# A hybrid decoder step on one core: another order for the end of the QKV projection, the attention loop and the start of the output projection

## The chip, the core and the metric

The kernel runs on one core of a Trainium2 chip. The core has five engines, each working through its own instructions in order: TensorE (PE, with its weight loads shown as PEld), VectorE (DVE), ScalarE (ACT), GpSimd (POOL) and SyncE (SP). DMA transfers are issued from the queues of SP, ACT and POOL and run beside the engines. The metric is the device time of one execution in microseconds (us), as the median of several.

## The reference, cut to what matters

One inference step of a two-layer decoder: a prompt of 512 tokens and 8 sample sequences of 8 tokens with a past of 2048, D = 1024. Layer 0 is attention in three head groups `gi` with (window, dilation) = (128, 1), (512, 4), (2048, 16); layer 1 is a state-space (SSM) layer; each is followed by a SwiGLU feed-forward (FFN).

```python
qkv = (h @ w_qkv).reshape(B, T, 3, N_DIL, N_HEAD_SLOTS, HEAD_DIM)
q = rope(rmsnorm(qkv[:, :, 0], q_gain), pos)
k = rope(rmsnorm(qkv[:, :, 1], k_gain), pos)
v = qkv[:, :, 2]
...
s = jnp.einsum('bqhd,bqkhd->bqhk', q_blk, kf) * (HEAD_DIM ** -0.5)   # keys at distance 0, d, .., window
s = jnp.where(valid, s, -jnp.inf); lse = logsumexp(s); p = exp(s - lse)
o = jnp.einsum('bqhk,bqkhd->bqhd', p, vf)
...
wts = softmax(stack(lses)); o = sum over groups of wts * o           # merged per head slot
return o @ w_o, new_bufs
```

For the samples the old keys and values come from caches in HBM; new keys and values go to output caches. Everything is float32: a product is three TensorE products of high and low halves, high x high, high x low and low x high.

## The kernel before, in words

**Projection.** `qkv_phase` computes the nine chunks of `CHUNKS`, each a (part, group) of 512 columns with part 0 = q, 1 = k, 2 = v; the last is (2, 1). A chunk has four steps of two 128-row slices of `w_qkv`, so there are 36 steps, numbered j = 0 to 35 (`turn[0]`). In a step (`qkv_chunk`) TensorE runs six 128x512 matmuls for each of four tiles t = 0..3 of prompt rows and four for t = 4, the sample rows, into five accumulators `acc`. After each tile a `slot()` runs whatever was put there with `later(ahead, fn)`, `ahead` slots on; a step has five slots.

At the start of step j `begin()` puts on SP's queue, in this order: the weights of step j+2; the cached keys that `SCORES[j]` lists by group (0 or 1), to be worked on in step j; the pairs that `PAIRS` lists for step j+1. A pair is a tile of cached keys of group 2 and the queries spread over 128 partitions (`kc<-qscr`), 512 KB each; VectorE multiplies and reduces them one step later into a table P. Every fourth pair completes a sequence, and `Close2.turn` transposes P. `begin` also splits the weights of step j+1 into `whi` (ScalarE) and `wlo` (VectorE). The tiles of keys and pairs come from one pool, `kst`, of six buffers.

Keys of groups 0 and 1 are transposed on TensorE (`Score.turn`, into `pt`), copied by ScalarE (`ks`), and multiplied with the queries (`Score.dots`). All decode scores pass through one PSUM bank `Sd`; a row of it is 128 old keys and 8 new ones, and it is evicted with mask and maximum by VectorE:

```python
v.tensor_tensor_reduce(Sall[:, self.b, self.gi, :], Sd, md[:, self.gi, :], 1.0, -3e38, OP.add, OP.max, mx3[:, self.b, self.gi:self.gi + 1])
```

There are 24 such rows, eight sequences by three groups. `Kept` keeps all these operations in program order on their engine; because it records them, they all bear its line (L688) in the profile.

**Attention.** `attn_phase` loops over n = 0..19. For n < 16 it takes block n of the prompt (head pair n // 4, row class n % 4): `scores` (into `S`), `masked` (VectorE), `exps` (ScalarE), one turn later `turn` and `evict` (transposes through `pt` into P0 and P12), one more turn later `values`: products P12 with the values of groups 1 and 2 (`vt[1]`, `vt[2]`), and at the end of a head pair P0 with those of group 0 (`vt[0]`) and the reciprocal denominators R. `att` is a ScalarE copy of the values, multiplied by R on VectorE. Two turns carry one sample sequence (`Decode`): softmax, transposes, then products with 13 tiles of cached values (`cache_tile`, loaded through SP into `kst` and four more buffers) and one of new values `vn`.

**Output.** `wo_phase` splits `att` into `ath` (ScalarE) and `atl` (VectorE), multiplies with `w_o` in four chunks of 256 columns (`mm6`: six 128x288 matmuls for each slice) and adds the residual `xr`, read back from HBM in one load, into `xT`. Three pairs of banks `acc` take turns. FFN 0 follows, with `ssm_setup` beside it, whose loads (`ssm_a_re`, `ssm_log_dt`, `ssm_c_re` as `cw`, `ssm_b_re` as `bw`) stand on SP's queue around that of `xr`. Operations that are not kept in order are put in order by a scheduler.

The functions around it, with the profile's line numbers:

Of the kernel before, what the change touches and what calls it, by code (L numbers as in the profile page):

```python
# [18 lines left out]
D = 1024  # L19
T = 512  # L20
# [31 lines left out]
def _build(nc, tc, A, es):  # L52
# [71 lines left out]
    with ExitStack() as qs:  # L124
# [7 lines left out]
        md = dsp.tile([128, 3, 136], BF16, name="md")  # L132
        kst = rs_.enter_context(right("kst", bufs=KST))
# [80 lines left out]
    with ExitStack() as p3:  # L214
        wo_phase(nc, tc, A, p3, locals())
# [117 lines left out]
def qkv_chunk(nc, L, x, begin, step, pre=None, slot=None):  # L333
# [7 lines left out]
    for kk in range(4):  # L341
        wh, wl = begin()
        for t in range(4):
            if pre is not None:
                pre(kk, t)
            for k2 in range(2):
                k = kk * 2 + k2
                ah, al = x.h[:, k, t * 128:(t + 1) * 128], x.l[:, k, t * 128:(t + 1) * 128]
# [5 lines left out]
        for k2 in range(2):  # L354
            k = kk * 2 + k2
            mm(ps[4], x.s[:, k, :], wh[:, k2, :], start=k == 0, stop=False)
            mm(ps[4], x.s[:, k, :], wl[:, k2, :], start=False, stop=k == KT - 1)
        if slot is not None:
            slot()
# [32 lines left out]

class Close2:
    def __init__(self, nc, L, v, dk, psp, nm, P, b):
        self.nc, self.L, self.v, self.psp, self.nm, self.P, self.b = nc, L, v, psp, nm, P, b
# [7 lines left out]
    def turn(self):  # L403
# [8 lines left out]
        self.v.tensor_tensor_reduce(L["Sall"][:, b, 2, :], Sd, L["md"][:, 2, :], 1.0, -3e38, OP.add, OP.max, L["mx3"][:, b, 2:3])  # L412


def qkv_phase(nc, tc, A, es, L):
# [77 lines left out]
    def begin():  # L493
# [25 lines left out]
        for b, part, kc, qb in due:  # L519
# [6 lines left out]
            if part == 3:  # L526
                c = Close2(nc, L, v, dk, psd, "Sd", prods.pop(b), b)
                later(10, lambda c=c: close(c))
        return splits.pop(0)

    class Score:
# [23 lines left out]
        def dots(self, us):  # L555
# [14 lines left out]
            v.tensor_tensor_reduce(Sall[:, self.b, self.gi, :], Sd, md[:, self.gi, :], 1.0, -3e38, OP.add, OP.max, mx3[:, self.b, self.gi:self.gi + 1])  # L570
# [20 lines left out]
    def qk_chunk(gi, part):  # L591
# [17 lines left out]
        def finish(t, ahead):  # L609
# [9 lines left out]
            if t == 4 and part == (gi < 2):  # L619
# [23 lines left out]
    def v_chunk(gi, wk, vt=None):  # L643
        ps = qkv_chunk(nc, L, x, begin, step, None, slot)
        for t in range(5):
# [9 lines left out]
            kv_out(nc, A, gi, 1, t, a)  # L655

# [12 lines left out]
    def values():  # L669
        nc.sync.dma_start(vt0, L["vtscr"].rearrange("t p c -> p t c"))  # L670
        nc.sync.dma_start(mp, A["c_mp"])

    notes[34] = values
    with ExitStack() as e4:
        v_chunk(1, e4.enter_context(pool("wk2")), vt1)
# [3 lines left out]
    return [vt0, vt1, vt2], mp  # L679
# [11 lines left out]
def attn_phase(nc, tc, A, es, L):  # L691
# [20 lines left out]
    den, rd, S2, PT, sm, P0, P12, O = {}, {}, {}, {}, {}, {}, {}, {}  # L712

    def scores(n):
# [4 lines left out]
        for b in range(4):  # L719
            for h in range(2):  # L720
                o, k = S2[n][h][b * 32:b * 32 + 32, 0:256], kT[0][half[h], hp, max(b - 1, 0) * 128:(b + 1) * 128]
                if not b:
                    o, k = o.rearrange("p (a c) -> p a c", a=2), k[:, None, :].to_broadcast([64, 2, 128])
                mm(o, qT[0][half[h], hp, r * 128 + b * 32:r * 128 + b * 32 + 32], k, start=True, stop=True, tile_position=(h * 64, b * 32))
        sl = slice(r * 128, r * 128 + 128)
        for gi in (1, 2):
            for h in range(2):
                mm(S2[n][h][:, (gi + 1) * 128:(gi + 2) * 128], qT[gi][half[h], hp, sl], kT[gi][half[h], hp, sl], start=True, stop=True)
# [7 lines left out]
    def exps(n, h):  # L736
        x, nm = sm[n][h]
        s.activation(x, x, AF.Exp, bias=nm, scale=-1.0, accum_out=den[n // 4][:, n % 4, h:h + 1])
# [23 lines left out]
    def values(n):  # L762
# [8 lines left out]
        if r < 3:  # L771
            return
        for b in range(4):
# [6 lines left out]
        R = pS.tile([128, 512], F32, name="S")  # L780
        for c in range(4):
            for j in range(4):
                mm(R[j * 32:j * 32 + 32, c * 128:c * 128 + 128], rd[hp][:, c, j // 2:j // 2 + 1].to_broadcast([128, 32]), ident,
                   start=True, stop=True, tile_position=(0, j * 32))
        av = att[:, hp, :T].rearrange("p (b i r) -> p r b i", b=4, r=4)
        s.activation(av, o_, AF.Copy)
        v.tensor_tensor(av, av, R.rearrange("p (r b i) -> p r b i", r=4, b=4), OP.mult)
# [3 lines left out]
    class Decode:  # L791
        def __init__(self, b):
            self.b, self.u = b, 0
            P = Sall[:, b].rearrange("p a b -> p (a b)")
            nm, dn, rd = (dk.tile([128, 1], F32, name=x, bufs=2) for x in ("dnm", "ddn", "drd"))
            v.tensor_reduce(nm, mx3[:, b, :], AX.X, OP.max)
            v.tensor_scalar(nm, nm, -SCALE, None, op0=OP.mult)
            s.activation(P, P, AF.Exp, bias=nm, scale=SCALE, accum_out=dn)
            v.reciprocal(rd, dn)
            v.tensor_scalar(P, P, rd, None, op0=OP.mult)  # L800
            self.pw = dk.tile([128, 24], F32, name="pw")
            v.tensor_copy(self.pw.rearrange("p (a b) -> p a b", a=3), Sall[:, b, :, 128:136])
            self.vn = dk.tile([24, 512], F32, name="vn", bufs=2)
            nc.sync.dma_start(self.vn, dram(vscr, b * 8 * 512, [[64 * 512, 3], [512, 8], [1, 512]]))
# [19 lines left out]
        def values(self, part):  # L824
            b, Z = self.b, Pz[self.b % 2]
            if part == 0:
                self.O = pD.tile([128, 128], F32, name="Sd")
                for hp in range(4):
                    mm(self.O[hp * 32:hp * 32 + 32, :], self.pn[:, hp * 32:hp * 32 + 32], self.vn[:, hp * 128:hp * 128 + 128], start=True, stop=False, tile_position=(0, hp * 32))
            for gi, c0 in (((0, 0), (1, 0), (1, 2)), ((2, 0), (2, 2), (2, 4), (2, 6)))[part]:  # L830
                w = min(2, UNITS[gi] - c0)
                turns[0] += 1
                vc = cache_tile(nc, A, kst if turns[0] % 10 < KST else kp, "kc", gi, b, c0, w, 1)
                for c in range(w):
                    for hp in range(4):
                        pz = self.pa[:, hp, :] if self.u == 0 else Z[:, self.u - 1, hp, :]
                        mm(self.O[hp * 32:hp * 32 + 32, :], pz, vc[:, c, hp * 128:hp * 128 + 128], start=False, stop=self.u == 12, tile_position=(0, hp * 32))
                    self.u += 1
            if part == 0:
                return  # L840
            self.os = dk.tile([128, 128], F32, name="os")
# [9 lines left out]
    dec = {}  # L851
    for n in range(20):
# [643 lines left out]
```

## Time and profile before

| what | us |
|---|---|
| median of 3 runs (lowest, highest) | 1522.9 (1522.62, 1525.23) |
| the profiled execution | 1525.21 |
| its span, first to last instruction | 1523.4 |
| projection, by the trace | 0 to 319.5 |
| attention loop | 319.5 to 418 |
| output projection begins | 419.5 |
| mean granted TensorE clock | 0.993 of full |

How to read the rows that follow. Waits are "engine tile line <- engine tile line that released it: us in total, times, longest". Time rows are "start, length, engine, line, operation, out<-in", then partitions by elements and types, how many like it stand together, and in brackets the idle time before and who ended it. A stretch has busy time and count of each engine, then granted clock, busy share of the 16 DMA engines, and GB/s. A DMA row names the queue and, where it is a group, KB each and us from issue to landing.

### The profile page before, as it was taken

Reading aid. Unit: us, or ns where it says so; the run is one execution under the profiler, and the core shown is the slowest. Engines: PE = TensorE matmul, PEld = TensorE weight load, DVE = VectorE, ACT = ScalarE, POOL = GpSimd, SP = SyncE. Lnnn points to the kernel's source line nnn. Section 1 sums busy time; section 2 is a strip of 40 time slices with the busy share of each in tenths; the row PEclk is TensorE's granted clock in tenths of the full one; section 3 lists DMA queues with packets and bytes.
Section 4 is the critical chain, followed back from the end, with each engine's and each line's share of the span. In section 5 each row is a group of like instructions: output and inputs, shape, how many; then the busy total and the mean of one; then the engine's idle time right before and its main releaser. Section 6 shows DMA issues by size and latency. Waiting matters only on the chain. (4 is left out here: it accounts for less than half of the span.)

```text
span 1523.4 us, 29540 instructions
## 1 busy us (share of the span) xinstructions
PE 1480.0 (97%) x12406; PEld 1388.4 (91%) x12406; DVE 910.8 (60%) x1507; ACT 520.9 (34%) x790; POOL 315.2 (21%) x369
## 2 busy tenths in 40 slices
PE   9999999789999999999999999999999999999998
PEld 7877777557799999999999999899999999999998
DVE  5899988545467853688887568754443333333332
ACT  4523445345553221222123363432332212221222
POOL 2021132310031019544434330020110001000100
PEclk9999999979999999999999999999999999999999
DMA  7568587979775555797666828865546555442222
GB/s 253 190 242 299 187 288 236 345 261 311 256 231 191 194 199 195 243 302 257 240 242 238 301 97 252 267 206 191 190 164 221 190 191 192 149 151 89 83 63 76
DMA packets 190460, 322.62 MB, mean 212 GB/s; under 512 B 39480, under 2 KB 137016, under 8 KB 188792
## 3 DMA queue, kind: packets, MB, share of 16 engines
q1 hardware_dynamic: 182808, 303.63, 58.3%
q10 hardware_dynamic: 4992, 10.04, 1.9%
q0 software_dynamic: 2528, 7.08, 1.3%
q8 instruction: 97, 1.59, 0.4%
q14 instruction: 35, 0.29, 0.1%
HBM read 289.22 MB, written 118.78 MB: 268 GB/s over the span
## 5 line engine op out<-in xcount | busy, mean ns | idle before, releaser
L107 PE MATMUL acc<-xgl,whi 128*128 128x288 f32 x1760 | 378.6, 296 | 1.0 <-DVE xgl L172 1.0
L107 PE MATMUL acc<-xgh,wlo 128*128 128x288 f32 x1760 | 377.7, 296 | 0.0
L107 PE MATMUL acc<-xgh,whi 128*128 128x288 f32 x1760 | 377.1, 296 | 0.1
L101 DVE TENSOR_TENSOR wlo<-raw,whi 128x1024 fp32r<-128x1024 f32 (+1 forms) x168 | 207.6, 1236 | 238.1 <-ACT whi L100 234.8
L100 ACT ACTIVATE whi<-raw 128x1024 fp32r<-128x1024 f32 (+1 forms) x168 | 174.5, 1039 | 458.6 <-PE acc L107 404.8
L107 PEld LDWEIGHTS acc<-xgl,whi 128*128 128x128 f32 x1760 | 282.6, 188 | 2.5 <-DVE xgl L172 1.3
L107 PEld LDWEIGHTS acc<-xgh,wlo 128*128 128x128 f32 x1760 | 282.7, 188 | 0.6 <-issue 0.2
L107 PEld LDWEIGHTS acc<-xgh,whi 128*128 128x128 f32 x1760 | 281.8, 188 | 0.5 <-DVE gt L933 0.3
L935 POOL TENSOR_TENSOR gt<-gt,rstd 128x576 f32<-128x576 f32 x44 | 77.1, 1754 | 431.1 <-ACT gt L934 431.0
L107 PE MATMUL acc<-hh,whi 128*128 128x288 f32 x704 | 151.4, 296 | 0.0
L107 PE MATMUL acc<-hh,wlo 128*128 128x288 f32 x704 | 151.2, 295 | 0.0
L107 PE MATMUL acc<-hl,whi 128*128 128x288 f32 x704 | 151.0, 295 | 0.0
L337 PE MATMUL acc<-whi,xh 128*128 128x512 f32 x288 | 119.7, 417 | 1.2 <-ACT a L688 0.7
L107 PEld LDWEIGHTS acc<-hh,wlo 128*128 128x128 f32 x704 | 113.2, 188 | 0.2 <-issue 0.2
L107 PEld LDWEIGHTS acc<-hl,whi 128*128 128x128 f32 x704 | 113.0, 188 | 0.2 <-issue 0.2
L337 PE MATMUL acc<-wlo,xh 128*128 128x512 f32 x288 | 113.1, 394 | 0.0
L107 PEld LDWEIGHTS acc<-hh,whi 128*128 128x128 f32 x704 | 113.1, 188 | 0.0
L337 PE MATMUL acc<-whi,xl 128*128 128x512 f32 x288 | 112.3, 395 | 0.0
L192 POOL TENSOR_TENSOR ssum<-ssum,sq 128x576 f32<-128x576 f32 x21 | 36.2, 1723 | 232.4 <-ACT sq L191 232.4
L337 PEld LDWEIGHTS acc<-whi,xh 128*128 128x128 f32 x288 | 54.6, 190 | 12.3 <-ACT a L688 1.7
L337 PEld LDWEIGHTS acc<-whi,xl 128*128 128x128 f32 x288 | 54.6, 190 | 12.1
L947 DVE TENSOR_TENSOR xT<-acc,xT 128x576 f32<-128x576 f32 x48 | 36.2, 754 | 48.1 <-PE acc L107 48.1
(362 smaller groups left out, 2015.9 us busy)
## 6 DMA issues: line engine op xcount, KB each, us to landing
o_kv_s<-cache_kv_w SPq DMA_DIRECT2D x64, 1020.0 KB, 7.5
kc<-cache_kv_w SPq DMA_DIRECT2D x96, 512.0 KB, 6.7
raw<-ffn_w_gate SPq DMA_DIRECT2D x44, 512.0 KB, 3.6
raw<-ffn_w_up SPq DMA_DIRECT2D x44, 512.0 KB, 3.6
raw<-ffn_w_down SPq DMA_DIRECT2D x40, 512.0 KB, 3.4
raw<-w_qkv SPq DMA_DIRECT2D x36, 512.0 KB, 6.5
kc<-qscr SPq DMA_DIRECT2D x32, 512.0 KB, 6.1
o_kv_s<-cache_kv_w SPq DMA_DIRECT2D x16, 1008.0 KB, 6.1
```

Source lines behind the costliest of these rows:

```text
L100: s.activation(hi, raw, AF.Copy)
L101: mark[0] = v.tensor_tensor(lo, raw, hi.bitcast(F32), OP.subtract)
L107: te.matmul(ps[:, c, :HN], w, x[:, c * HN:(c + 1) * HN], start=first and i == 0, stop=last and i == 2)
L192: g.tensor_tensor(self.ss, self.ss, sq, OP.add)
L337: ins = nc.tensor.matmul(*a, **kw)
L935: g.tensor_tensor(t, t, nin.r, OP.mult)
L947: v.tensor_tensor(xv, ps[m][:, :, :HN], xv, OP.add)
```

## The change

It does six things. ScalarE copies a row of `Sd` to SBUF, and VectorE masks it there. `PAIRS` and `SCORES` get other numbers, and two sequences of group 0 share one load. In the last chunk the sample rows go first, each tile is evicted right behind its last matmul, and between the evictions stand the softmax of sequence 0 and the scores, masks and exponentials of block 0 (in the projection's `pt` banks and two `kst` tiles). The mask `mp` and the values `vt0` are loaded in steps 34 and 35 after everything else; new values `vn` are loaded from POOL's queue and multiplied last. Two of the four `w_o` loads are put at n = 11 and 13, the denominators' copy and the last sequence's output go ahead of the P0 products. And the output projection begins with all high parts of its first chunk, with `xr` in four loads; two copies of `ssm_setup` are held behind it.

```diff
-PAIRS = {7: 1, 9: 1, 10: 1, 11: 1, 12: 2, 13: 2, 14: 2, 15: 2, 17: 1, 18: 1, 19: 1, 21: 1, ... 31: 1, 32: 2, 33: 2, 34: 2}
+PAIRS = {7: 1, 8: 1, 10: 1, 11: 1, 12: 2, 13: 2, 14: 1, 15: 1, 18: 1, 19: 1, 20: 1, ... 23: 2, ... 27: 2, ... 31: 2, 32: 2, 33: 2, 34: 1}
...
+def row_out(v, s, L, Sd, b, gi):
+    o = L["Sall"][:, b, gi, :]
+    s.activation(o, Sd, AF.Copy)
+    v.tensor_tensor_reduce(o, o, L["md"][:, gi, :], 1.0, -3e38, OP.add, OP.max, L["mx3"][:, b, gi:gi + 1])
...
-                later(10, lambda c=c: close(c))
+                later(6 if j > 31 else 10, lambda c=c: close(c))
...
-        nc.sync.dma_start(vt0, L["vtscr"].rearrange("t p c -> p t c"))
-        nc.sync.dma_start(mp, A["c_mp"])
-    notes[34] = values
+    notes[34] = lambda: kept(nc.sync.dma_start(mp, A["c_mp"]))
+    notes[35] = lambda: kept(nc.sync.dma_start(vt0, L["vtscr"].rearrange("t p c -> p t c")))
...
+    def then(t):
+        if t == 4:
+            row_soft(v, s, Sall, mx3, 0, *soft)
+        if t == 0:
+            ...
+            score_block(lambda *a, **kw: kept(te.matmul(*a, skip_group_check=True, **kw)), S0, qT, kT, 0)
+            ...
+            for h in range(2):
+                v.tensor_tensor_reduce(sm0[h][0], S0[h], mp[:, 0, :], -SCALE, 3e38, OP.add, OP.min, sm0[h][1])
+        if t == 2:
+            for h in range(2):
+                s.activation(sm0[h][0], sm0[h][0], AF.Exp, bias=sm0[h][1], scale=-1.0, accum_out=den0[:, 0, h:h + 1])
...
-        v_chunk(1, e4.enter_context(pool("wk2")), vt1)
+        v_chunk(1, e4.enter_context(pool("wk2")), vt1, (4, 0, 1, 2, 3), then)
...
-        s.activation(av, o_, AF.Copy)
-        v.tensor_tensor(av, av, R.rearrange("p (r b i) -> p r b i", r=4, b=4), OP.mult)
+        s.activation(av, R.rearrange("p (r b i) -> p r b i", r=4, b=4), AF.Copy)     # ahead of the P0 products
+        between()
...
+        v.tensor_tensor(av, av, o_, OP.mult)
...
-            nc.sync.dma_start(self.vn, dram(vscr, b * 8 * 512, [[64 * 512, 3], [512, 8], [1, 512]]))
+            g.dma_start(self.vn, dram(vscr, b * 8 * 512, [[64 * 512, 3], [512, 8], [1, 512]]))
...
+    wo = L["split_w"](raws[0], s, v)
+    dec[7].values(1)
+    values(15, dec[7].out)
...
-    xr = wk.tile([128, KT, NT], F32, name="xr")
-    nc.sync.dma_start(xr, L["xscr"])
+    xr = []
+    for c in range(4):
+        xr.append(wk.tile([128, 2, NT], F32, name=f"xr{c}"))
+        nc.sync.dma_start(xr[c], L["xscr"][:, 2 * c:2 * c + 2])
...
+        if c == 0:
+            for parts, x in (((wh, wl), ath), ((wh,), atl)):
+                for m, k in ...:
+                    for w in parts: ...     # both 128-column tiles: all of ath, then all of atl
```

What this does to the order, at three places. First SP's queue at the end of the projection, in steps 33 to 35; before:

```order
L389 DMA kc<-cache_kv_w 128x512 x2
L389 DMA kc<-cache_kv_w 128x2x512
L670 DMA vt_2805<-vtscr 128x4x512
L508 DMA kc<-qscr 128x1024
L671 DMA mp<-c_mp 128x2048
L389 DMA kc<-cache_kv_w 128x2x512
L508 DMA kc<-qscr 128x1024
L88 DMA raw<-w_o 128x4x256
L389 DMA kc<-cache_kv_w 128x512 x2
```

and now:

```order
L505 DMA raw<-w_qkv 128x2x512
L513 DMA kc<-cache_kv_w 128x2x512
L390 DMA kc<-cache_kv_w 128x2x512
L521 DMA kc<-qscr 128x1024
L690 DMA mp<-c_mp 128x2048
L691 DMA vt_2853<-vtscr 128x4x512
L390 DMA kc<-cache_kv_w 128x512
L390 DMA kc<-cache_kv_w 128x2x512 x6
```

The values `vt0` and the mask went behind the last pair (the last `kc<-qscr`), step 34 has one pair instead of two, and no `w_o` load is left here; three of them stood right above the first fence. Second, VectorE in steps 34 and 35, before:

```order
L688 TENSOR_TENSOR kc<-kc 128x1024
L101 TENSOR_TENSOR wlo<-raw,whi 128x1024
L688 TENSOR_REDUCE P_2930<-kc 128x2x4x2
L688 TENSOR_TENSOR kc<-kc 128x1024
L688 TENSOR_REDUCE P_2930<-kc 128x2x4x2
L688 ISA Sall,mx_77<-Sd,md 128x136
```

and now:

```order
L747 TENSOR_TENSOR kc<-kc 128x1024
L747 TENSOR_REDUCE P_2886<-kc 128x2x4x2
L747 ISA Sall,mx_77<-Sall,md 128x136
L747 ISA mx_77 128x1
...
L747 SCALAR_TENSOR_TENSOR a<-acc,rr,ks 64x512
L747 TENSOR_REDUCE f_82<-mx_77 128x1
```

The row's mask (ISA) still stands behind the products, but reads `Sall` in SBUF and no longer the bank `Sd`; the last rows are the sample rows' eviction and the softmax of sequence 0. Third, SP's queue at the start of the output projection, before:

```order
L1048 DMA raw<-ssm_a_re 32x128
L1049 DMA raw<-ssm_a_im 32x128
L880 DMA xr<-x_scr 128x4608
L1051 DMA ldt<-ssm_log_dt 32x2
L1054 DMA cw<-ssm_c_re 128x8x64
L1055 DMA cw<-ssm_c_im 128x8x64
L1057 DMA bw<-ssm_b_re 128x32x16
L1058 DMA bw<-ssm_b_im 128x32x16
```

and now:

```order
L1120 DMA raw<-ssm_a_re 32x128
L1121 DMA raw<-ssm_a_im 32x128
L1123 DMA ldt<-ssm_log_dt 32x2
L1127 DMA cw<-ssm_c_re 128x8x64
L1128 DMA cw<-ssm_c_im 128x8x64
L1130 DMA bw<-ssm_b_re 128x32x16
L1131 DMA bw<-ssm_b_im 128x32x16
L939 DMA xr_5039<-x_scr 128x1152
```

The residual `xr`, in four loads, went from ahead of `cw` and `bw` to behind them.

More of the change, by code (lines that the diff above doesn't have):

```diff
@@ L330, in prep, with qkv_chunk @@
                 self.roots()
-def qkv_chunk(nc, L, x, begin, step, pre=None, slot=None):
+def qkv_chunk(nc, L, x, begin, step, pre=None, slot=None, order=range(5), ends=None):
     acc = L["acc"]
@@ L342, in qkv_chunk @@
         wh, wl = begin()
-        for t in range(4):
+        for t in order:
             if pre is not None:
@@ L353, in qkv_chunk @@
                 slot()
[L354 to L359, printed above, removed]
+            if ends is not None and kk == 3:
+                ends(ps, t)
         step()
@@ L641, in qk_chunk, with v_chunk, ends @@
             works.setdefault(turn[0] + i, []).append(lambda t=t, ahead=4 if (gi, part, t) == (0, 1, 3) else ahead: finish(t, ahead))
-    def v_chunk(gi, wk, vt=None):
-        ps = qkv_chunk(nc, L, x, begin, step, None, slot)
-        for t in range(5):
+    def v_chunk(gi, wk, vt=None, order=range(5), then=None):
+        def ends(ps, t):
             if t == 4:
@@ L655, in v_chunk @@
             kv_out(nc, A, gi, 1, t, a)
+            if then is not None:
+                then(t)
+        if then is None:
+            ps = qkv_chunk(nc, L, x, begin, step, None, slot)
+            for t in range(5):
+                ends(ps, t)
+        else:
+            qkv_chunk(nc, L, x, begin, step, None, slot, order, ends)
     for part, gi in CHUNKS[:8]:
@@ L718, in scores @@
         S2[n] = [pS.tile([128, 512], F32, name="S") for _ in range(2)]
[L719 to L728, printed above, removed]
+        score_block(mm, S2[n], qT, kT, n)
     def masked(n):
@@ L760, in evict, with values @@
             v.reciprocal(rd[hp], den[hp])
-    def values(n):
+    def values(n, between=lambda: None):
         hp, r = divmod(n, 4)
@@ L772, in values @@
             return
+        R = pS.tile([128, 512], F32, name="S")
+        for c in range(4):
+            for j in range(4):
+                mm(R[j * 32:j * 32 + 32, c * 128:c * 128 + 128], rd[hp][:, c, j // 2:j // 2 + 1].to_broadcast([128, 32]), ident,
+                   start=True, stop=True, tile_position=(0, j * 32))
+        av = att[:, hp, :T].rearrange("p (b i r) -> p r b i", b=4, r=4)
+        s.activation(av, R.rearrange("p (r b i) -> p r b i", r=4, b=4), AF.Copy)
+        between()
         for b in range(4):
@@ L849, in out @@
                 v.tensor_copy(att[half[h], :, q0:q0 + 8], ot[half[h], :, h * 8:h * 8 + 8])
-    dec = {}
-    for n in range(20):
-        if n < 16:
+    dec, raws = {0: Decode(0)}, []
+    for n in range(17):
+        if n in (11, 13):
+            raws.append(L["ring"].tile([128, 4, 256], F32, name="raw", bufs=4))
+            tc.keep_in_program_order(nc.sync.dma_start(raws[-1], dram(A["w_o"], len(raws) * 256 - 256, [[D, 128], [128 * D, 4], [1, 256]])))
+        if 0 < n < 16:
             scores(n)
@@ L856, in attn_phase @@
             turn(n - 1)
-        if n < 16:
+        if 0 < n < 16:
             masked(n)
@@ L881, in wo_phase @@
     ath = wk.tile([128, 4, NT], F32R, name="ath")
     atl = wk.tile([128, 4, NT], F32R, name="atl")
+    kv_, ks = Kept(tc, v), Kept(tc, s)
     for k in range(4):
-        s.activation(ath[:, k], att[:, k], AF.Copy)
-        v.tensor_tensor(atl[:, k], att[:, k], ath[:, k].bitcast(F32), OP.subtract)
+        ks.activation(ath[:, k], att[:, k], AF.Copy)
+        kv_.tensor_tensor(atl[:, k], att[:, k], ath[:, k].bitcast(F32), OP.subtract)
+    ws = [L["wo"][0], split_w(L["wo"][1], ks, kv_)]
     for c in range(4):
-        wh, wl = load_w(A["w_o"], D, 0, 4, c * 256, 256, 0.0)
+        if c > 1:
+            ws.append(split_w(fetch_w(A["w_o"], D, 0, 4, c * 256, 256, 0.0)))
+        wh, wl = ws[c]
+        ps = [acc() for _ in range(2)]
+        if c == 0:
+            for parts, x in (((wh, wl), ath), ((wh,), atl)):
+                for m, k in ((m, k) for m in range(2) for k in range(4)) if x is atl else ((m, k) for k in range(4) for m in range(2)):
+                        for w in parts:
+                            for h in range(2):
+                                tc.keep_in_program_order(te.matmul(ps[m][:, h, :HN], w[:, k, m * 128:(m + 1) * 128], x[:, k, h * HN:(h + 1) * HN],
+                                                                   start=x is ath and k == 0 and w is wh, stop=x is atl and k == 3))
@@ L897, in wo_phase @@
             n0.add(2 * c + m)
+    return last
 THIRDS = ((0, 4), (4, 8), (8, 11))
```

132 lines of the change are left out of this document (82 added, 50 removed).

## The prediction

> **What bounds the kernel now.** I read the page first: TensorE is busy nearly all the time.
>
> ```profile
> PE 1480.0 (97%) x12406; PEld 1388.4 (91%) x12406; DVE 910.8 (60%) x1507; ACT 520.9 (34%) x790; POOL 315.2 (21%) x369
> ```
>
> So the ceiling of any change that keeps the matmuls is PE's idle time plus what a lowered clock costs. Second view, busy time in stretches; columns after the length are PE, PEld, DVE, ACT, POOL, the granted clock, the DMA share and GB/s.
>
> ```profile
> core 0: us, PE busy (x) PEld busy (x) DVE busy (x) ACT busy (x) POOL busy (x), PEclk, DMA share, GB/s
> 0.00:80.00 80.00, 77.56 (x368) 63.81 (x369) 56.81 (x113) 39.68 (x60) 9.97 (x24) 1.00 0.61 211
> 80.00:160.00 80.00, 76.49 (x374) 61.40 (x373) 76.53 (x90) 30.39 (x44) 13.38 (x35) 1.00 0.81 283
> 160.00:270.00 110.00, 108.52 (x868) 84.78 (x867) 94.03 (x139) 54.36 (x86) 28.01 (x71) 1.00 0.71 237
> 270.00:300.00 30.00, 25.48 (x195) 19.62 (x196) 15.20 (x22) 9.70 (x15) 11.47 (x27) 1.00 0.98 346
> 300.00:315.00 15.00, 7.56 (x38) 5.86 (x37) 6.46 (x9) 1.43 (x2) 0.37 (x2) 0.66 0.89 321
> 315.00:335.00 20.00, 16.75 (x211) 10.85 (x210) 9.51 (x36) 13.49 (x32) 6.02 (x8) 0.83 0.63 214
> 335.00:415.00 80.00, 76.81 (x1811) 60.90 (x1807) 38.44 (x159) 42.23 (x131) 0.00 (x0) 1.00 0.87 302
> 415.00:425.00 10.00, 8.29 (x123) 7.84 (x112) 4.29 (x7) 3.70 (x6) 0.00 (x0) 0.83 0.66 219
> 430.00:600.00 170.00, 170.00 (x1279) 169.59 (x1278) 111.60 (x239) 54.31 (x64) 54.02 (x62) 1.00 0.56 195
> ```
>
> From 430 on PE has no gap and the change touches nothing, so all of it must happen before. Losses against a PE that never waits at full clock, as length minus busy, plus busy times (1 − clock): 270–300: 4.52; 300–315: 7.44 idle and 7.56 × 0.34 = 2.6 of clock; 315–335: 3.25 and 16.75 × 0.17 = 2.85; 335–415: 3.19; 415–425: 1.71 and 1.41. That is 27.0 us; 0–270 holds another 7.4.
>
> Third view, the waits of TensorE in 270–320, and the time order behind the largest:
>
> ```profile
> PE Sd L563 <- DVE mx L688: 9.5, 3, 7.4
> ...
> 301.25 1.22 DVE L688 TENSOR_TENSOR kc<-kc 128x1024 f32<-128x1024 f32 x1 [7.84 <-DMA kc<-qscr]
> 305.23 1.23 DVE L688 TENSOR_TENSOR kc<-kc 128x1024 f32<-128x1024 f32 x1 [0.49 <-DMA kc<-qscr]
> 306.49 1.22 DVE L688 TENSOR_REDUCE P<-kc 128x16 f32<-128x1024 f32 x1
> 307.63 0.29 DVE L688 CUSTOM_DVE_ANT_0 Sall<-Sd,md 128x136 f32<-128x136 f32 x1
> 308.07 0.66 PE L563 MATMUL Sd<-ks,Qy 128*32 128x128 f32 x8 [7.44 <-DVE mx L688]
> ```
>
> PE waits 7.44 for the single score bank Sd. Its eviction takes 0.29, but stands on in-order DVE behind two products whose loads landed at 301.25 and 305.23. So PE waits for a DMA that it does not need. Afterwards the clock is low: 5-us stretches of the same view.
>
> ```profile
> 290.00:295.00 5.00, 3.93 (x37) 2.87 (x37) 2.08 (x8) 0.15 (x1) 2.18 (x6) 1.00 1.08 367
> 300.00:305.00 5.00, 0.64 (x3) 0.19 (x1) 3.49 (x3) 1.06 (x1) 0.37 (x2) 0.86 1.05 385
> 305.00:310.00 5.00, 1.93 (x19) 1.74 (x20) 2.97 (x6) 0.00 (x0) 0.00 (x0) 0.50 1.06 374
> 320.00:325.00 5.00, 3.04 (x42) 1.70 (x35) 3.13 (x8) 2.88 (x5) 3.07 (x4) 0.91 0.98 341
> 325.00:330.00 5.00, 4.98 (x37) 3.13 (x36) 2.43 (x10) 3.67 (x13) 0.77 (x1) 0.50 0.18 66
> ```
>
> With 1.07 of 5 idle (290) the clock stays 1.00; after 1.96 idle (320) it is 0.50. I count a drop only where idle reaches about 0.4 of a stretch.
>
> **The change, part by part.** *Score bank to ScalarE (24 rows).* Nearest row, same bank, 128 columns:
>
> ```profile
> 329.40 0.27 ACT L688 ACTIVATE pa<-Sd 128x128 f32<-128x128 f32 x1
> ...
> 289.09 1.06 ACT L688 ACTIVATE whi<-raw 128x1024 fp32r<-128x1024 f32 x1 [2.30 <-DMA raw<-w_qkv]
> 315.12 1.84 ACT L688 ACTIVATE vt<-acc,rr 128x512 f32<-128x512 f32 x3
> ```
>
> 24 × 0.28 = 6.7 us on an engine 34% busy: hidden, as long as ACT is not itself stuck (rival 3). Queued behind such a copy on ACT are the key copies (ks), the weight copies (whi) and the evictions, each up to 0.28 later; PE waits for them, but has other products of the step meanwhile. DVE's mask and maximum stay, but nobody on PE waits for them. What still can wait for DVE on PE is a sum of key-query products: Close2's transpose stands six slots after the sum's step begins, in the last steps, instead of ten.
>
> *Loads in other steps.* The queue of SP around the stall:
>
> ```profile
> 281.08 4.34 SPq L88 DMA_DIRECT2D raw<-w_o  x3
> ...
> 288.92 0.38 SPq L670 DMA_DIRECT2D vt<-vtscr  x1
> 289.40 1.34 SPq L508 DMA_DIRECT2D kc<-qscr  x1
> 290.78 0.42 SPq L671 DMA_DIRECT2D mp<-c_mp  x1
> 294.59 0.33 SPq L508 DMA_DIRECT2D kc<-qscr  x1
> ```
>
> Three w_o loads (0.52 MB each by their shapes), vt (1.05) and mp (0.52) stand ahead of the last pair and go behind it, and step 34 has one pair instead of two (1.05 MB less): 4.2 MB at the 385 GB/s of row 300–305 is 10.9 us earlier at most; 0 at least, if it is the six buffers, freed by PE and DVE, that hold the queue, and not bytes. The wait of 7.44 thus ends between 0 and 7.44; I take 1.0, near the low end, because both causes (order on DVE, late bytes) are hit. With it the idle share stays small, so 2.6 of clock return.
>
> The other waits of 270–300 (4.52) have many causes; I take 3.0 left. A new one is in it: the last chunk starts with the sample rows, whose accumulator is freed by ScalarE's fourth copy of the chunk before, behind a score copy. The copies take 1.84 / 3 = 0.61 each: 4 × 0.61 + 0.28 = 2.7, while PE has four matmuls of the sample rows and a score beside it, about 1.2, so 1.5 is new. Term 270–315: 1.5 + 6.4 + 2.6 = **10.5**; ends 14.6 (all) and 3.9 (rival 1).
>
> *0–270.* Pairs leave steps 9, 14, 15, 17 and 34 for 8, 20, 23, 27 and 31. A pair is 1.22 + 1.22 = 2.44 on DVE. A step is some 8.5 us, so 80–160, with DVE at 76.5 of 80, loses four and gets easier, and 160–270 gains four: from 94.0 to some 104 of 110, nearly full. PE lost 3.5 in the one and 1.5 in the other: I take **0**, ends ±2.
>
> *First softmax within the projection.* Before, attention begins with a chain that PE sits out:
>
> ```profile
> 322.48 0.66 PE L688 MATMUL S<-kT,att 64*32 64x256 f32 x14 [1.08 <-DVE nm L688]
> ...
> 324.67 1.97 PE L688 MATMUL pt<-ident,sm 128*128 128x128 f32 x8 [0.88 <-ACT sm L688]
> ```
>
> The scores, masks and exponentials of block 0 now run beside the last chunk's matmuls, and the evictions that follow the last matmul (315.12 above) are spread over it. What is late next is the last value copy on ACT, which now stands behind two exponentials, and then the transposes of block 0, whose bank it clears: I take 1.5 left of 3.25 + 2.85, so **4.6**; ends 6.1 and 0 (the drop at 325 comes again). On that drop the Trainium skill, "TensorE: Matmul & The Clock Gate", Part 4, says that transposes do not count as PE-busy in the same way; attention opens with transposes, so by it the drop recurs (rival 5). The row 335–415 holds the same transposes, block after block, at 1.00, so I go by the row. Part 1 of that page asks for an idle window of some 3.4 us before the clock halves; the trace halves it at 325 after waits of 1.1 at most, so I keep the 0.4.
>
> *Attention loop.* New values (vn) come last, and their load goes from SP's queue to POOL's. On SP it waited for the store of the new values, with all value tiles behind it:
>
> ```profile
> SPq L804 <- DMA vscr<-a: 7.5, 1, 7.5
> ```
>
> On POOL it stands behind the last stores of values; POOL is idle in 335–415, and the wait, if it remains, holds only vn's product at the end of a sequence. PE did not wait for the value tiles before (3.19 idle in 80), so little is to be had: I take **0.5**; ends 3.2 and −2 (w_o, 2.1 MB, now loads inside the loop: 5.4 us at 385, in a stretch whose share is 0.87 already).
>
> *Output.* Before:
>
> ```profile
> 419.46 1.68 PE L107 MATMUL acc<-ath,whi 128*128 128x288 f32 x6 [1.25 <-ACT ath L884]
> ...
> 426.92 0.43 PE L107 MATMUL acc<-ath,whi 128*128 128x288 f32 x2
> 427.19 0.42 PE L107 MATMUL acc<-atl,whi 128*128 128x288 f32 x2
> ...
> 419.75 4.37 SPq L1055 DMA_DIRECT2D cw<-ssm_c_im  x1
> 424.16 3.13 SPq L1057 DMA_DIRECT2D bw<-ssm_b_re  x1
> 427.33 3.05 SPq L1058 DMA_DIRECT2D bw<-ssm_b_im  x1
> ```
>
> High parts first takes away the wait for low parts, and the last attention values need one product behind them instead of a copy and a product; the first 128x288 matmul still waits for one product and one copy, so of 1.71 + 1.41 I leave 1.6: **1.5**. Its cover: xr now stands on SP behind cw and bw, 10.55 us of issue in the rows, of which a part is there only because xr's 2304 KB stood ahead (9.1 to landing, its row stands below). Those loads begin with the last block's sparse products, 45 small products before the last attention value: 45 × 76.81 / 1811 = 1.9. Then four small issues (an estimate of 0.4 each by the 0.33 to 0.42 of SP's rows above, 1.6), 4.4 to 10.55 for the rest, and 2.3 for a quarter of xr: it lands 6.4 to 12.6 after the last attention value. PE can go on without it for three accumulators of 24 matmuls, which start 0.27 a pair: 72 × 0.134 = 9.6, and 1 at the start. The worst stall is 12.6 + 0.6 (the sum into xT, half of the 1.22 of a 128x1024 product) − 10.6 = 2.6. Ends of the term: 3.1 and 1.5 − 2.6 − 1.4 of clock = −2.5 (rival 2). DVE's copy of the step sizes (ldt) now stands behind the last sum into xT; nothing on PE needs it before.
>
> ```profile
> xr<-x_scr SPq DMA_DIRECT2D x1, 2304.0 KB, 9.1
> ```
>
> Sum: 10.5 + 0 + 4.6 + 0.5 + 1.5 = **17.1 us**. The profiled execution took 1525.2 (span 1523.4 and 1.8 around it), 2.3 over the median of 1522.9. So the profile would show about 1508.1; against the median the time is 1505.8, told as 1506.
>
> **Rivals.** 1: the last pair is late all the same, since SP waits for buffers. The transpose of the last sum then holds PE some 5 us in step 35 and the clock falls: 4.0 + 2.6 less, gain 10.5, 1512.4. For: the load issued at 289.40 was there at 301.25, after 11.9. Against: the last pair now has the better part of two steps between its issue and its sum's transpose.
>
> 2: xr behind the small packets stalls PE 2.6, with 1.4 of clock as in 415–425: gain 13.1, 1510. The Trainium skill, "DMA: Bandwidth & Descriptors", Specifications, asks for at least 512 B per transfer for line rate; bw has runs of 64 B. The rows above show 3.1 us for the issue of 256 KB of bw, which agrees.
>
> 3, slower: ScalarE takes DVE's place as the blocker. Its weight copy waits in order for w_qkv (2.30 above), and the score copy behind it holds PE. With the four steps of the last chunk each losing more than 17.1 / 4 = 4.3, the kernel is slower; at 7.44 each, as for Sd now, 29.8 − 17.1 = 12.7 over, 1536. For: the DMA share is 0.98 to 1.08 there, and weight loads are in that queue. Against: 3.7 MB of w_o, vt and mp leaves that place, and the wait shown is 2.30.
>
> 4: bytes bound the whole of 270–430. The rows give 30 × 346 + 15 × 321 + 20 × 214 + 80 × 302 + 10 × 219, and 1.0 MB for the 5 us left: 46.8 MB. In 160 − 17 us that is 327 GB/s. If no more than the loop's 302 can be sustained, it takes 155, gain 5, 1518. Against: 346 was held over 270–300.
>
> 5: the clock halves again as attention begins, although the waits are short, because its opening work is transposes: 2.85 less, gain 14.2, 1508.7. For: 0.50 at 325 after waits of 1.1 at most; against: 1.00 over 335–415. It is the case that the page's Part 4 above would make.
>
> **How the numbers follow.** Forecast 0.46, rival 1 0.15, rival 2 0.10, rival 4 0.12, rival 5 0.09, rival 3 0.06; 0.02 for something within 0.2% of before, which is about what a measurement of this kernel can tell from no change. Forecast and rivals 1, 2, 4 and 5 are faster, less some 0.03 of rival 4's tail: faster 0.88, same 0.05, slower 0.07. The forecast's own range is 1500 to 1510: the ends above the terms (4.1, 2, 1.5, 2.7, 1.6) put together as independent make 5.7, those below without rivals 1 and 2 (2, 3, 2.5, some 1) make 4.5. The stated range reaches from a little under that to rival 4's 1518, and leaves out rival 3, no change, and the tails.
>
> **What would show it.** Right: no wait of PE for Sd over 1.5 us; granted clock 1.00 through 270–330; PE idle under 5 us between 270 and the end of the projection; attention's first transposes waiting under 0.5 us; the first output matmul under 1.2 us. Wrong: a wait of the sum's transpose for DVE in step 35, waits of Sd for ACT with w_qkv behind them, xT's first sum waiting for xr, or waits for kc through the attention loop.

## The result, and the profile after

The changed kernel takes 1506.53 us (median of 4 runs, 1503.49 to 1508.09) against 1524.07 for the kernel before in the same runs: a ratio of 0.9882, 95% interval 0.9862 to 0.9902. The profiled execution has a span of 1504.8, 18.6 under the one before. Its stretches, in the columns known from above:

```profile
270.00:300.00 30.00, 28.99 (x247) 22.25 (x236) 19.03 (x37) 12.89 (x25) 10.95 (x28) 1.00 1.02 367
300.00:315.00 15.00, 14.84 (x200) 10.53 (x198) 7.16 (x29) 11.86 (x30) 7.21 (x10) 1.00 0.81 276
315.00:335.00 20.00, 18.36 (x428) 14.37 (x426) 9.23 (x38) 9.77 (x31) 1.12 (x2) 1.00 0.94 312
335.00:400.00 65.00, 60.49 (x1450) 47.76 (x1450) 31.77 (x128) 35.11 (x103) 2.23 (x4) 1.00 0.91 307
400.00:410.00 10.00, 9.30 (x70) 9.33 (x71) 4.34 (x6) 3.85 (x6) 0.00 (x0) 1.00 1.10 180
410.00:420.00 10.00, 8.30 (x63) 8.10 (x62) 9.04 (x17) 5.69 (x9) 3.00 (x2) 1.00 1.00 331
```

Where 300–315 had 7.44 idle and a clock of 0.66, there is 0.16 and 1.00; the loop's stretches, 335–400, now hold 4.5 idle in 65. TensorE's waits in 240–330:

```profile
PE O L747 <- issue: 1.2, 1, 1.2
PE acc L338 <- ACT a L747: 1.0, 1, 1.0
PE Sd L747 <- DVE Sall L747: 0.4, 1, 0.4
PE pt L747 <- ACT vt L747: 0.2, 1, 0.2
```

No wait for the score bank is left in the projection: the first, the third and the fourth row belong to the attention loop. ScalarE's copy of a row and VectorE's mask stand far apart now; some of their rows and of the products', in the order of time:

```profile
281.28 0.29 ACT L747 ACTIVATE Sall<-Sd 128x136 f32<-128x136 f32 x1 [0.16 <-PE Sd L417]
284.79 1.23 DVE L747 TENSOR_TENSOR kc<-kc 128x1024 f32<-128x1024 f32 x1 [2.41 <-DMA kc<-qscr]
286.95 0.29 ACT L747 ACTIVATE Sall<-Sd 128x136 f32<-128x136 f32 x1 [1.19 <-PE Sd L581]
288.94 0.28 ACT L747 ACTIVATE Sall<-Sd 128x136 f32<-128x136 f32 x1 [1.70 <-PE Sd L581]
289.96 0.29 DVE L747 CUSTOM_DVE_ANT_0 Sall<-Sall,md 128x136 f32<-128x136 f32 x1
```

The products' loads are still late (VectorE waits 2.41). The masks follow in the order of the copies, so the one at 289.96 belongs to the copy of 281.28, the first row, and comes 8.7 after it began: that is a wait which PE no longer has.

Three points, the same in every trace, give a ledger: the first score matmul of the loop (S), the first matmul of the output projection (ath), and the sum over FFN 0's norm (ssum). The changed kernel does 1.3 us of the loop's scores in the last chunk, ahead of S; `a_softmax_late`, `a_chunk_old` and `a_combined` do not. The three columns are of the one profiled execution, the last is the median of all.

| run | S | S to ath | ath to ssum | time, median |
|---|---|---|---|---|
| before | 319.5 | 99.9 | 34.0 | 1524.07 |
| after | 305.9 | 94.8 | 34.4 | 1506.53 |
| b_act_evict | 318.2 | 101.7 | 34.0 | 1524.73 |
| b_new_tables | 317.9 | 104.0 | 32.7 | 1523.86 |
| b_both | 307.4 | 101.2 | 34.2 | 1518.47 |
| a_dve_evict | 318.6 | 95.4 | 32.9 | 1518.52 |
| a_old_tables | 310.6 | 97.9 | 32.7 | 1513.47 |
| a_wo_early | 311.1 | 93.0 | 35.4 | 1509.6 |
| a_softmax_late | 305.3 | 94.5 | 32.6 | 1505.86 |
| a_chunk_old | 304.8 | 102.6 | 33.1 | 1511.11 |
| a_xr_first | 305.6 | 96.3 | 31.8 | 1506.46 |
| a_half_values | 307.3 | 90.5 | 32.9 | 1502.15 |
| a_combined | 304.6 | 96.5 | 32.4 | 1508.11 |

Of 18.6, the projection gave 13.6 and does 1.3 more; the loop gave 5.1, of which those 1.3; the output lost 0.4. Up to the end of step 31 the two differ by 0.2 (that step's sample rows begin at 268.8 and 268.6).

### The profile page after: what moved, and what is told of

It reads as the page before. It is cut to its first block, busy times and chain, and to the rows that moved or that the text cites. A ratio compares the mean times of both kernels' runs of the same rounds, so it can differ in the third digit from the quotient of the medians.

```text
span 1504.8 us, 29545 instructions
## 1 busy us (share of the span) xinstructions
PE 1471.7 (98%) x12406; PEld 1382.3 (92%) x12406; DVE 909.9 (60%) x1507; ACT 526.1 (35%) x814; POOL 322.3 (21%) x377
## 3 DMA queue, kind: packets, MB, share of 16 engines
q8 instruction: 97, 1.59, 0.4%
## 5 line engine op out<-in xcount | busy, mean ns | idle before, releaser
L1006 ACT ACTIVATE gt<-gt 128x576 f32<-128x576 f32 x44 | 30.2, 686 | 100.2 <-DVE gt L1005 94.5
```

The source lines that it names most:

```text
L1006: s.activation(t, t, AF.Silu)
```

## Experiments

### Two parts, each undone and each done alone

`b_` stands for the kernel before with something added, `a_` for the changed kernel with something undone. VectorE evicts again:

```diff
-    s.activation(o, Sd, AF.Copy)
-    v.tensor_tensor_reduce(o, o, L["md"][:, gi, :], ...)
+    v.tensor_tensor_reduce(o, Sd, L["md"][:, gi, :], ...)
```

> The changed kernel with one part undone: VectorE again evicts a score row straight from the bank Sd, with mask and maximum in one. Theory 'order' (the stall came from the eviction's place behind the products on VectorE): PE waits for Sd again in the last four steps. If that place alone was the cause, 7 us or more of the 14.7 gained there come back: about 1514, with a lower clock after the stall. Theory 'late loads' (the stall came from the loads that the products wait for, which now land earlier): no more than the waits that VectorE's masks show now. In the changed kernel the second score of step 34 ended on PE at 288.84, and VectorE reached the first mask at 289.96: about 2 to 3 us, no drop of the clock, about 1509.

Measured: 1518.52 (ratio to before 0.9953, 0.9931 to 0.9975). 12 of 17.5 come back, but more than half of it early. The largest wait, in step 25, with the eviction that it waited for:

```profile
210.96 0.29 DVE L746 CUSTOM_DVE_ANT_0 Sall<-Sd,md 128x136 f32<-128x136 f32 x1
...
211.40 1.08 PE L575 MATMUL Sd<-ks,Qz 128*32 128x128 f32 x16 [5.98 <-DVE mx L746]
```

VectorE, fuller here with the moved pairs, reached the eviction late, and by step 28 the kernel is 7.1 behind the changed one. In 270–322 there are three more:

```profile
PE Sd L575 <- DVE mx L746: 4.1, 3, 1.8
```

From the sample rows of step 31 to S the run loses 3.8, where "order" expected 7 or more in the last four steps: it has the direction, but the larger part of the loss stands around the wait in step 25, which neither theory named. "Late loads", 1509 without a lower clock, is refuted: the clock halves at 208 and again at 290. (It took the mask at 289.96 for that of the score just before it.)

```diff
-PAIRS = {7: 1, 8: 1, ...}; SCORES = {21: (1,), ...}     # of the change, with its shared load
+PAIRS = {7: 1, 9: 1, ...}; SCORES = {22: (1,), ...}     # of the kernel before, one sequence a load
-                later(6 if j > 31 else 10, ...)
+                later(10, ...)
```

> The changed kernel with the other part undone: PAIRS and SCORES as before (two pairs in step 34, one group-0 sequence for each load, ten slots before the transpose of a sum); ScalarE's copy, the late loads of the mask and of vt0, and all else stay. 'Order': PE does not wait for VectorE's queue any more, so under 2 us are lost: below 1508.5. 'Late loads': the pairs of step 34 land late again and the transposes of keys or of the last sum wait for them: 4 to 8 us lost, 1511 to 1514, with a lower clock in the last chunk.

Measured: 1513.47 (0.9928, 0.9909 to 0.9947): 7 lost; in the trace S comes 4.7 later, the loop takes 3.1 more and the stage behind it 1.7 less. The size is that of "late loads", its mechanism is not: the clock stays at 1.00 and no wait for a load stands in 270–325. PE is idle 3.1 between the sample rows of step 31 and S, where it was 1.0; 1.6 were lost before that. The waits there, but for one of 0.5:

```profile
PE pt L695 <- ACT ks L742: 1.3, 1, 1.3
PE S L742 <- ACT Sall L742: 0.7, 1, 0.7
PE acc L339 <- ACT a L742: 0.7, 1, 0.7
```

So each part is worth 7 to 12 when it is taken away, but with the w_o loads in the loop and the mask and `vt0` behind, the old tables bring no wait for late pairs back to PE. Now each one put alone into the kernel before:

```diff
-        self.v.tensor_tensor_reduce(L["Sall"][:, b, 2, :], Sd, ...)      # and the same in Score.dots
+        row_out(self.v, self.s, L, Sd, b, 2)
```

> The kernel before with one part done alone: ScalarE copies each row out of Sd, VectorE masks it in SBUF. 'Order': the wait of 7.44 and the clock after it go: 9 to 10 us faster, about 1514. 'Late loads': the wait moves to the next thing that needs the products, the transpose of the last sum in step 35, or the weight split behind the products: under 4 us faster, about 1521.

> The kernel before with the other part done alone: PAIRS, SCORES, the shared load of group 0, six slots before a sum's transpose in the last steps, the mask's load in step 34 and vt0's in step 35, both kept last; VectorE still evicts Sd itself, and the w_o loads stay where they were (three ahead of the last pair, 1.6 MB). 'Late loads': 7 us or more faster, 1517 or less. 'Order': PE still waits for Sd behind VectorE's products, 4 us or less faster, 1520 or more.

Measured: 1524.73 (0.9999, 0.9983 to 1.0015) and 1523.86 (0.9994, 0.9979 to 1.0008). Neither gives anything. With ScalarE's copy alone, step 34 runs on without a wait for Sd, and then PE stands for the next cached keys (those that `SCORES` lists for step 34; TensorE works on them in step 35):

```profile
300.67 1.22 DVE L694 TENSOR_TENSOR kc<-kc 128x1024 f32<-128x1024 f32 x1 [7.12 <-DMA kc<-qscr]
...
309.51 1.12 PE L557 MATMUL pt<-ident,kc 128*128 128x128 f32 x4 [4.53 <-DMA kc<-cache_kv_w]
```

The keys are late like the pairs; both come through SP's queue, at a DMA share of 1.04 to 1.05. By its own waits the queue also stood for buffers, 2.9 for VectorE's products and 2.1 for the transposes in 280–312, and bytes and buffers are not parted here. With the tables alone the bytes come in time, but PE waits for Sd behind VectorE's work, once early and four times late:

```profile
211.37 1.08 PE L568 MATMUL Sd<-ks,Qz 128*32 128x128 f32 x16 [4.85 <-DVE mx L690]
...
PE Sd L568 <- DVE mx L690: 5.7, 4, 2.4
```

Then both, in the kernel before:

```diff
+PAIRS, SCORES, row_out, later(6 if j > 31 else 10, ...)
+    notes[34] = lambda: kept(nc.sync.dma_start(mp, A["c_mp"]))
+    notes[35] = lambda: kept(nc.sync.dma_start(vt0, ...))
```

> The kernel before with both parts together that gave nothing alone: ScalarE's copy of a score row, and the tables with the late loads of mask and vt0. The last chunk's order, the attention loop and the output are as before, and the scheduler still puts three w_o loads ahead of the last pair. Theory 'two causes in a row' (the eviction behind VectorE's products, and the late loads of pairs and keys; each alone is enough to hold PE): now the long wait of the last steps goes, 9 to 14 us faster, 1510 to 1515. Rival 'w_o' (1.6 MB of w_o ahead of the last pair are the late bytes): PE then waits some 5 us more in step 34 or 35, for cached keys or for the last sum, and less than 6 us are gained: 1518 or more. Rival 'last chunk' (its new order is what the two parts need): no gain, 1522 or more.

Measured: 1518.47 (0.9956, 0.9938 to 0.9973). By the ledger the projection is 12.2 shorter, where the parts alone made 1.3 and 1.6. By the time 6.7 are left, where the parts alone made nothing and 0.8: the effect lies in the two together, as "two causes in a row" says, but it is less than the 9 to 14 forecast. The nine runs spread from 1513.31 to 1522.8, with the profiled one at the fast end (1515.62), and the loop takes 1.3 more. The number fits the rival "w_o" as well (1518 or more), and its wait for the last sum is there, at half its size. What waits are left:

```profile
301.71 0.30 PE L412 MATMUL Sd<-ident,P 128*128 128x128 f32 x1 [2.67 <-DVE P L696]
311.08 0.66 PE L696 MATMUL S<-kT,att 64*32 64x256 f32 x14 [1.88 <-DVE nm L696]
...
321.04 0.42 PE L696 MATMUL Sd<-vn,pn 24*32 24x128 f32 x8 [1.65 <-DMA vn<-vscr]
```

The last sum still waits for its pair, 2.67, the masks wait for VectorE, and the new values, first in their group of products, for their load.

### The place of w_o

```diff
-        if n in (11, 13): ...                                 # two w_o loads in the loop
-    ws = [L["wo"][0], split_w(L["wo"][1], ks, kv_)]
+    ws = []                                                   # all four by the scheduler
```

> The changed kernel with one part undone: the w_o loads are all left to the scheduler again, which puts three of them ahead of the last pair, and one split of w_o ahead of VectorE's work in step 34, one ahead of the loop's first evictions. 'w_o' theory: 5 us or more lost before the attention loop, 1511 or more. 'Two causes in a row' without w_o: 1.6 MB at 385 GB/s are 4.2 us of delay for the pair, of which the six slots of cover hide most: under 2 us lost there; the loop, with 2 MB less in it, gains 1 to 2 us: about as now, 1505 to 1508.

Measured: 1509.6 (0.9905, 0.9887 to 0.9923), 3.1 more than the change. S comes 5.1 later, as the "w_o" theory has it (5 or more); the loop is 1.8 shorter, as its rival has it (1 to 2); and the time lies between the two. In the last chunk:

```profile
298.16 1.22 DVE L747 TENSOR_TENSOR kc<-kc 128x1024 f32<-128x1024 f32 x1 [5.57 <-DMA kc<-qscr]
299.49 1.23 DVE L100 TENSOR_TENSOR wlo<-raw,whi 128x1024 fp32r<-128x1024 f32 x1
...
301.99 0.30 PE L414 MATMUL Sd<-ident,P 128*128 128x128 f32 x1 [2.10 <-DVE P L747]
```

```profile
300.00:305.00 5.00, 3.01 (x15) 2.09 (x15) 3.55 (x11) 2.41 (x4) 0.40 (x1) 0.75 0.92 310
```

A split of w_o stands on VectorE between the last product and its sum (1.23), the product's load was late, PE waits 2.10, and the clock falls (0.75 in 300–305). It is both the bytes and the place on VectorE; the run does not part them.

### The head of the loop

```diff
-        if t == 0: ...      # scores and masks of block 0
-        if t == 2: ...      # its exponentials
-        if 0 < n < 16:      # scores, masked, exps
+        if n < 16:
```

> The changed kernel with block 0's scores, masks and exponentials back at the head of the attention loop (sequence 0's softmax stays in the last chunk). The work is the same, so what is lost is waiting and clock. My theory: PE idles some 2.5 us more at the start of the loop, as before, and the clock halves for some 5 us, another 2.6: about 4 to 5 us, 1511. Rival 'idle only': the idle comes back and the clock stays at 1.00, since no wait is over 1.3 us: 2 to 3 us, 1509. Rival 'covered': the sample rows' early eviction and the spread copies were what mattered: under 1 us.

Measured: 1505.86 (0.9877, 0.9854 to 0.99), nothing lost; the clock stays at 1.00 through the loop. The third theory holds, "covered". Then the last chunk put back as well:

```diff
-        v_chunk(1, ..., vt1, (4, 0, 1, 2, 3), then)
+        v_chunk(1, ..., vt1)
+        row_soft(v, s, Sall, mx3, 0, *soft)                   # behind the chunk
```

> The changed kernel with the softmax of block 0 back in the attention loop and the last chunk as before: tiles in the order 0 to 4, sample rows last, all evictions behind the chunk, the softmax of sequence 0 behind them. Against the run with only block 0's softmax put back (1505.9), theory 'spread evictions' (what took the wait and the low clock out of the loop's start is that the sample rows and the copies are done before the loop's masks): the loop's first masks wait for VectorE and ScalarE again, 2 to 3 us of idle, and the clock may fall for 2 to 3 more: 1508 to 1511. Rival (it was the w_o split that stood there on VectorE and ScalarE before): within 1 us, 1506.

Measured: 1511.11 (0.9915, 0.9892 to 0.9937): 5.2 over the run before it, the top of what "spread evictions" forecast; the profiled execution is one of the longer ones, 1513.45. The chain at the head of the loop, VectorE, then PE, then a stretch:

```profile
305.71 0.74 DVE L748 SCALAR_TENSOR_TENSOR a<-acc,rr,ks 64x512 f32<-64x512 f32 x1 [5.34 <-ACT ks L748]
307.95 1.60 DVE L748 TENSOR_SCALAR Sall<-Sall,f 128x408 f32<-128x408 f32 x1
...
310.84 0.78 PE L748 MATMUL S<-kT,att 64*32 64x256 f32 x14 [4.16 <-DVE nm L748]
```

```profile
310.00:315.00 5.00, 4.16 (x34) 3.29 (x34) 3.04 (x9) 2.67 (x8) 1.99 (x3) 0.66 0.73 240
```

The sample rows' eviction and the softmax of sequence 0 stand on VectorE ahead of the loop's first masks, PE waits 4.16, and the clock follows. Part of the 4.16 belongs to my putting the softmax of sequence 0 there; in the kernel before it stood behind the first masks, and a w_o split of 1.23 stood ahead instead. So the run shows that the place of this work on VectorE matters; what each piece of it is worth, no run shows.

### The loop's bytes and the residual

```diff
-                vc = cache_tile(..., c0, w, 1, ...)
+                vc = cache_tile(..., c0, 1 if gi == 2 else w, 1, ...)     # one unit, used for both
```

> The changed kernel with half of the cached values of group 2 left out: each of the 32 tiles loads one unit of 128 keys instead of two, and the products of both use it. 8.4 MB of some 29 less in the attention loop, the instructions on PE the same. Theory 'bytes' (the loop's waits, 5.6 us, put down to issue, come of DMA engines that are full): the loop's idle falls below 2 us and it is 4 us or more faster, about 1502. Rival 'instructions' (PE waits for something that no byte of data holds up): the idle stays within 1 us of 5.6.

Measured: 1502.15 (0.9859, 0.9825 to 0.9892), 4.4 faster; the intervals of the two ratios overlap, so the trace has to carry the point. The profiled execution is the longest of the four, 1509.88: far behind the loop, in 900–1000, its clock was 0.91, which cost some 8.5. The stretch of the loop without its ends, first after, then with half the values:

```profile
320.00:395.00 75.00, 69.93 (x1637) 55.42 (x1639) 37.27 (x149) 40.15 (x121) 2.79 (x5) 1.00 0.94 318
```

```profile
320.00:393.00 73.00, 70.53 (x1691) 56.00 (x1687) 37.86 (x155) 40.63 (x123) 3.35 (x6) 1.00 0.71 233
```

The idle goes from 5.1 to 2.5, the DMA share from 0.94 to 0.71. The expectation's 2 was missed by a little, its 4 us was met. The waits put down to issue, first after, then with half the values:

```profile
PE O L747 <- issue: 2.4, 3, 1.2
PE Sd L747 <- issue: 1.6, 2, 1.0
```

```profile
PE O L747 <- issue: 0.7, 1, 0.7
...
PE Sd L747 <- issue: 0.5, 1, 0.5
```

With one more of 0.4 after, they fall from 4.4 to 1.2 with the bytes alone, though no data releases them by the trace. The road can be read from the traces all the same. The page of either kernel lists a DMA queue q8 of kind "instruction", 97 packets with 1.59 MB, so 16 KB each, and in the loop one of them lands about every 6 us. Set beside their landing times, each of the six waits behind this 4.4 ends 1.3 to 1.5 after such a packet has landed, and so do the two with half the values and the five before the change. So PE, as far as the timing shows, stands for its own next instructions, which come through DMA queues beside the data. What holds the packet up, no run shows: once it has begun it takes about 1 us with either amount of data.

```diff
+            with tc.issue_after(L["xrmark"].ins):             # each load of the SSM setup
                 nc.sync.dma_start(...)
```

> The changed kernel with the four loads of xr put ahead of all loads of the SSM setup on SP's queue. Theory 'small packets' (xr lands 11.5 us after the last attention value because cw and bw stand ahead of it): the wait of 1.70 of the output projection for xT goes, and VectorE's wait of 6.49 for xr shrinks to under 3; 1.7 us faster, 1504.8. Rival 'bytes': the DMA engines are full there (share 1.03 to 1.14), xr lands late all the same, within 1 us of now. Second rival: FFN 0 then waits for the SSM setup, which comes later, and loses more than 1 us.

Measured: 1506.46 (0.9877, 0.9853 to 0.9901), no change. The wait for xT is gone and the stage from ath to ssum takes 31.8 instead of 34.4. But this execution lost 1.5 in the loop and 2.5 behind ssum, 1.7 of these by a clock that halved for 3.41 at 964, and the stage took 32.6 with no wait for xT in a_softmax_late, where xr was not moved. So the wait comes and goes between executions, and whether the order of these loads pays stays open.

> A try at a faster kernel: the changed kernel with block 0's softmax left to the loop, xr ahead of the SSM loads, and the sample rows second instead of first in the last chunk, so that ScalarE has the time of one tile for the copy that the chunk's first matmul waited 1.0 for. From the runs of the parts: 0 to 1 from the softmax, 1.7 in the output stage, which the first trace gave back later, and 1.0 here: 1503 to 1506 by their sum; if each of these waits is covered by the next one, 1506 as now.

Measured: 1508.11 (1505.51 to 1510.71; 0.9896, 0.9878 to 0.9913). The chunk's first wait stayed at 1.0, on a prompt tile's accumulator instead of the sample rows'. No run with all the work in it beat the changed kernel by more than the runs spread.

## Why the prediction was right

The time was 1506.53 for 1506, and the stall that the prediction set out to remove is gone by the way it named. That the number is so near is luck: of the terms two were too small and two of the wrong sign, +4.4, +0.5, −2.4 and −1.9 against the forecast, and the errors nearly cancel. 14.9 + 5.1 − 1.9 − 0.4, and 0.9 that stand between these stretches, are the 18.6 of the spans, against 17.1. Of the signs named for "right", one failed: the first output matmul waits 1.39, not under 1.2; and one named for "wrong" came: the first sum into xT waits for xr.

*End of the projection, 10.5.* Measured: S is 13.6 earlier with 1.3 more work in front of it, 14.9, less the 0.4 that stood between the last matmul and S before. That is the upper end, 14.6. The step that was mis-sized is "I take 3.0 left" and "I take 1.0": from 269.4 to 305.9 PE is idle 1.0 in all, nearly all of it the one new wait that the prediction named (1.5 expected, 1.00 found). What the sum did not say is how the parts hang together. I treated the wait as one thing with two causes "both hit"; the four runs show two waits in a row, for which one cure alone is worth 1.3 to 1.6 in the traces and both 12.2 (0 to 0.8 and 6.7 by the times). Rival 1, that the last sum waits, came true only where the w_o loads were early: 2.10 in `a_wo_early`, 2.67 in `b_both`. Of rival 3 no row shows a sign: no wait of PE for Sd on ScalarE stands in 240–330.

*Steps before, 0.* Right: 0.2. But it rested on ScalarE's copy, which the prediction did not see: with VectorE evicting, the same tables cost 7 by step 28 and 9 by step 31.

*Head of the loop, 4.6.* Measured 5.1, first before, then after:

```profile
319.50:335.00 15.50, 12.64 (x172) 7.98 (x172) 8.89 (x32) 9.97 (x27) 3.84 (x4) 0.78 0.57 193
```

```profile
305.90:320.00 14.10, 13.55 (x273) 9.90 (x272) 7.00 (x32) 10.07 (x33) 5.26 (x7) 1.00 1.01 349
```

That is 2.86 of idle and 12.64 × 0.22 = 2.8 of clock before, 0.55 of idle and a full clock after, so rival 5 did not come. The size was right, the reason half wrong: the masks and exponentials of block 0 in the chunk gave nothing. What is left for it are the early sample rows, the spread copies and the absence of a w_o split; `a_chunk_old` shows that they matter together, not what each gave.

*Loop, +0.5.* Wrong in sign: 335–410 before held 3.2 idle, 320–395 after 5.1, so −1.9, near the end of −2. The step that failed is the choice of 0.5: w_o's 2 MB in the loop stood in the low end of the range and not in the term. In these stretches the DMA share went from 0.91 to 0.94, and the waits put down to issue are 4.4 with the w_o loads in the loop and 2.6 without (`a_wo_early`), which is its 1.8. Rival 4, bytes, was the right mechanism at a fifth of its price (2.4 under the forecast, where it takes 12.1). The load of `vn` from POOL's queue, for which the 0.5 stood, was not run by itself.

*Output, 1.5.* Measured −0.4, with a clock of 0.95 before and 1.00 after. "High parts first takes away the wait for low parts" had no row: no such wait stood in the trace before. The first copy still takes 1.39, and xr came where rival 2 put it:

```profile
404.75 3.57 SPq L939 DMA_DIRECT2D xr<-x_scr  x4
...
410.83 1.08 DVE L966 TENSOR_TENSOR xT<-acc,xr 128x288 f32<-128x288 f32 x2 [6.49 <-DMA xr<-x_scr]
...
412.19 0.50 PE L106 MATMUL acc<-ath,whi 128*128 128x288 f32 x2 [1.70 <-DVE xT L967]
```

The last attention product ended at 399.3, so xr landed 11.5 later (6.4 to 12.6 forecast) and cost 1.70 (2.6 at the worst). The Trainium skill, "DMA: Bandwidth & Descriptors", Specifications, wants 512 B per transfer for line rate. The trace agrees: in 400–410, with the loads of 64-B runs ahead, the DMA engines moved 180 GB/s at a share of 1.10, in 410–420 331 at 1.00. But the run that moved these loads shows no gain in time.

## What to carry to other kernels

A wait often has a second one right behind it: before a cure is called useless, look at what the waiting engine would meet next, and try the two together. Let an engine that has nothing late in its queue empty a single shared bank, and keep loads that nobody needs yet behind the last ones that somebody waits for. Moved bytes are paid somewhere: the w_o loads were worth 5.1 where they left and cost 1.8 where they went, by the traces, and 3.1 are left in the time.

## What the hardware showed

The clock changes in steps of one length. In each trace all its changes lie whole multiples of 3.41 us apart; before, it is at half from 303.58 for 10.24, from 324.06 for 6.83 and from 419.64 for 3.41. A drop thus costs at least 3.41 at half speed, 1.7 us of work. The Trainium skill, "TensorE: Matmul & The Clock Gate", Part 1, speaks of a free-running window of about 3.4 us, and the steps agree with it.

But the share of idle time in such a window does not decide alone, as I had taken it to do at 0.4. The window ahead of the drop at 324.06, and one of b_both with more idle time, behind which the clock stays at 1.00:

```profile
320.65:324.06 3.41, 2.05 (x28) 0.84 (x26) 2.48 (x8) 1.54 (x2) 2.13 (x3) 1.00 1.07 367
```

```profile
310.36:313.78 3.42, 1.82 (x26) 1.12 (x26) 1.50 (x6) 2.67 (x5) 3.25 (x4) 1.00 1.26 461
313.78:317.19 3.41, 2.73 (x34) 1.63 (x32) 2.33 (x8) 2.27 (x9) 0.60 (x1) 1.00 0.68 277
```

The first holds score products alone, on 64 rows; in the second full 128x128 transposes begin at 313.26. Whether that is the difference was not tried.

And in a_chunk_old VectorE's 128x408 operation took 1.60, while in the changed kernel it took 0.43:

```profile
302.16 0.43 DVE L747 TENSOR_SCALAR Sall<-Sall,f 128x408 f32<-128x408 f32 x1
```

In a_chunk_old POOL began to fill a tile at the same moment, 307.95, in two operations of 2.91 together; in the changed kernel POOL was busy 0.16 of the us from 302 to 303. Whether the fill stretched it was not tried.
